# Hard-max attention: dots and picks of tiles 120 to 123 ahead of the last two maxima, four-tile dots to tile 116, fp32 dots behind the key gathers, part of the one-hots on ScalarE

## The chip, the cores and the metric

One NeuronCore of one Trainium2 chip. The metric is the device time of one execution in microseconds; lower is better. Three executions of the kernel before took 440.21, 441.21 and 441.29 us. The granted TensorE clock was 0.96 to 0.97 in every run whose time is compared here. One group of runs was granted only 0.88 to 0.92 and took over a fifth longer, the kernel before too; it is used for no comparison of times.

## The reference

```python
# q, k, v: (4, 4096, 128) fp32, standard normal
logits = np.matmul(q, k.transpose(0, 2, 1))
best = np.argmax(logits, axis=-1)
return v[b_idx, best, :]
```

No softmax: each query takes the one row of `v` whose key has the largest product. So the kernel need not compute the products exactly; it has to find the right key.

## The kernel before

The 16384 queries are 128 tiles of 128 rows. For each tile a screen in fp16 runs over all keys, with matmuls on TensorE, `Abs` and `Relu` on ScalarE, and two VectorE instructions, `fold` (W, 1.30 us) and `top` (MAX8, 1.22 us). It gives the group of four keys that holds the largest product. The rest finds the key within the group:

- `gather` computes the index (`cand`), and GpSimd fetches the three key differences of each row by an indirect DMA (`kg`), one for each tile.
- `dots` multiplies and sums them on VectorE (`prod`, `p`, `D`), for two or four tiles at once.
- `pick` takes the best (`win`), with five small VectorE instructions for a chunk of tiles.
- `put_values` puts an indirect gather of `v` rows (`vr`) in the list of late gathers, one for each tile, and a store behind every fourth.

```python
def gather(c, t0, n):
    ...
    nc.vector.tensor_scalar(out=x, in0=TOP.bitcast(U32)[:, t0:t0 + n, 0], ...)          # cand
    for j in range(n):
        near_q.append(lambda j=j: nc.gpsimd.indirect_dma_start(out=kg[:, j]..., in_=k16[t0 // NQT],
                                                               in_offset=IOA(ap=x[:, j:j + 1], axis=0)))
    ...
def dots(c, x, m):
    ...
    for i in range(0, m, h):                                                           # h = 2 tiles
        nc.vector.tensor_tensor(out=prod[:, i:i + h], in0=kg[:, i:i + h], in1=natq..., op=OP.mult)
        yield gap
    nc.vector.tensor_tensor(out=p1, in0=prod[:, :, :, 0:64], in1=prod[:, :, :, 64:128], op=OP.add)
    yield gap
    nc.vector.tensor_tensor(out=p2, in0=p1[:, :, :, 0:32], in1=p1[:, :, :, 32:64], op=OP.add)
    yield "dve",
    nc.vector.tensor_reduce(out=d[:, x - c0:x - c0 + m, 1:4], in_=p2, axis=AX_X, op=OP.add)
```

At the end rows whose answer the screen leaves in doubt are packed together: `posn` gives their places, six one-hot matrices and six matmuls move their records (`fq_e`), from which come the group indices `gb_e` and the row `row_e`. Then three gathers of whole key groups in fp32 (FK) and one of queries (FQ), twelve exact products, a last gather of values (FV) and a scatter into the output, which has to wait for the last store. The last two tiles get whole fp32 dots at once (`xk`, `dots_whole`, `win_w`).

```python
def flags_last(t0, t1, ready, fill, late):
    ...
    for z in range(SLOTS):                                     # one-hots, SLOTS = 6
        nc.vector.tensor_scalar(out=OH[:, z], in0=iota_h, scalar1=posn[:, z:z + 1], ..., op0=OP.is_equal)
    for s in range(SLOTS):
        nc.tensor.matmul(out=ps2[:, 0:6], lhsT=OH[:, s, :], rhs=rec6[:, s, :], ...)
    fill()                                                     # dots_whole(0)
    ...                                                        # gb_e, rs_e, row_e
    late(LATE)                                                 # LATE pending value gathers
    get(FK[:, 0, :], ...); get(FQ, ...)
    for r in (1, 2): get(FK[:, r, :], ...)
    yield
    ...                                                        # exact dots, the remaining late gathers
    get(FV, v_flat, win, B * Sk)
    nc.gpsimd.indirect_dma_start(out=out_flat, out_offset=IOA(ap=rowk, axis=0), in_=FV, ...)

screen(T); top(T - 2); gathers(T - 2); flush()
fold(T - 1); late_now(1); top(T - 1); gathers(T - 1); flush()
end = flags_last(T // 2, T, last_picks, lambda: dots_whole(0), late_now)
next(end)
dots_whole(1); pick_whole()
for _ in end: pass
```

GpSimd takes its gathers in the order in which the program lists them; an index that is not ready holds up all that stand behind it.

Of the kernel before, what the change touches and what calls it, by code (L numbers as in the profile page):

```python
# [8 lines left out]
FP16 = mybir.dt.float16  # L9
# [6 lines left out]
OP = mybir.AluOpType  # L16
AF = mybir.ActivationFunctionType
# [4 lines left out]
TAU = 8.0  # L22
NEAR = 0.5
SLOTS = 6
LATE = 5
NKG = 6


# [1 line left out]
def kernel(ctx, tc, q, k, v, out):  # L30
    nc = tc.nc
    B, Sq, D = q.shape
    Sk = k.shape[1]
    P = 128
    NQT = Sq // P
    T = B * NQT
# [14 lines left out]
    fp = ctx.enter_context(tc.tile_pool(name="flag", bufs=1))  # L51
# [9 lines left out]
    kd = bp.tile([P, 2, 4, 3, P], FP16, name="kd", tag="kd")  # L61
# [18 lines left out]
    def put_first(b, h):  # L80
        if b >= B:
            return
        src = natk[b % 2][:, h].rearrange("p (g f) d -> p g f d", f=4)
        nc.vector.tensor_scalar(out=kd[:, h, :, 0, :], in0=src[:, :, 0, :], scalar1=-1.0, scalar2=None, op0=OP.mult)
        kb16 = k16[b].rearrange("(r x) d -> r (x d)", x=4).rearrange("(h p g) (f d) -> p h g f d", h=2, p=P, f=3)
        for f in range(3):
            nc.sync.dma_start(out=kb16[:, h, :, f, :], in_=kd[:, h, :, 0, :])
# [57 lines left out]
    iota_h = cp.tile([P, P], FP16, tag="iota_h")  # L145
# [5 lines left out]
    for h in range(2):  # L151
# [3 lines left out]
                            op0=OP.mult, op1=OP.add)  # L155
# [72 lines left out]
    def dpart(t, x):  # L228
        if t >= T:
            return  # L230
        ps = pp.tile([P, 1024], FP32, tag="u", name=f"pd_{t}_{x}")
        mm(ps, t, 1 + 2 * x, True)
        A = ep.tile([P, 1024], FP16, tag=f"A{x}", name=f"A_{t}_{x}")
        nc.scalar.activation(out=A, in_=ps, func=AF.Abs)  # L234
        A_t[t, x] = A

    def spart(t, x):
        if t < 0:
            return
        ps = pp.tile([P, 1024], FP32, tag="u", name=f"psn_{t}_{x}")  # L240
        mm(ps, t, 2 * x, False)
        A = A_t.pop((t, x))
        for n in range(2):
            nc.tensor.matmul(out=ps[:, n * 512:(n + 1) * 512], lhsT=identh, rhs=A[:, n * 512:(n + 1) * 512], start=False, stop=True)  # L244
        if x == 0:
            E = ep.tile([P, 1024], I16, tag="E", name=f"E_{t}")
            nc.scalar.activation(out=E, in_=ps, func=AF.Relu, scale=QSCALE)  # L247
            E_t[t] = E
        else:
            E_t[t] = (E_t[t], ps)  # L250

    def screen(t):
        dpart(t, 0)
        spart(t - 1, 0)
        dpart(t, 1)
        spart(t - 1, 1)
# [6 lines left out]
    def top(t):  # L263
        nc.vector.max(out=TOP[:, t, :], in_=W_t[t % NW].bitcast(FP32))  # L264
# [88 lines left out]
    def put_rec(t0, t1):  # L353
        nc.sync.dma_start(out=rec.rearrange("(p t) w -> p t w", t=T)[:, t0:t1, :], in_=TOP.bitcast(U32)[:, t0:t1, :])
# [111 lines left out]
    def flags_last(t0, t1, ready, fill, late):  # L466
# [18 lines left out]
        for r in range(1, 4):  # L485
# [5 lines left out]
                                op0=OP.is_ge, op1=OP.mult)  # L491
        posn = fp.tile([P, SLOTS], FP32, tag="posn", name="posn_e")
# [2 lines left out]
                                       scalar=-2.0 * Sk, in1=e8[:, 1:4, 0:SLOTS].rearrange("p r s -> p s r"),  # L495
                                       op0=OP.mult, op1=OP.add)
        OH = fp.tile([P, SLOTS, P], FP16, tag="OHe", name="OH_e")
        for z in range(SLOTS):
            nc.vector.tensor_scalar(out=OH[:, z], in0=iota_h, scalar1=posn[:, z:z + 1], scalar2=None, op0=OP.is_equal)
        ps2 = pp.tile([P, 1024], FP32, tag="u", name="fq_e")  # L500
        for s in range(SLOTS):
# [9 lines left out]
        def get(dst, src, idx, hi):  # L511
            nc.gpsimd.indirect_dma_start(out=dst, out_offset=None, in_=src, in_offset=IOA(ap=idx, axis=0),
                                         bounds_check=hi - 1, oob_is_err=False)

        late(LATE)
        get(FK[:, 0, :], k_flat, gb[:, 0:1], B * Sk)
# [39 lines left out]
    def gather_whole(t):  # L556
        i = t - (T - 2)
        if i == 0:
            X_t["c"] = sp.tile([P, 2], U32, tag="xc", name="xc", bufs=1)
        c = X_t["c"][:, i:i + 1]  # L560
        nc.vector.tensor_scalar(out=c, in0=TOP.bitcast(U32)[:, t:t + 1, 0], scalar1=IDX, scalar2=IDX | (B - 1) * Sk,
                                op0=OP.bitwise_and, op1=OP.bitwise_xor)
        kk = X_t[i] = fp.tile([P, 512], FP32, tag=f"xk{i}", name=f"xk{i}")
        near_q.append(lambda: nc.gpsimd.indirect_dma_start(out=kk, out_offset=None, in_=k_flat, in_offset=IOA(ap=c, axis=0)))

    def dots_whole(i):
        for f in range(4):
            pr = fp.tile([P, P], FP32, tag="xp", name=f"xp_w_{i}_{f}", bufs=2)
            nc.vector.tensor_tensor_reduce(out=pr, in0=X_t[i][:, f * P:(f + 1) * P], in1=q32[:, i, :], scale=1.0, scalar=0.0,
                                           op0=OP.mult, op1=OP.add, accum_out=XD[:, i, f:f + 1])  # L570
# [112 lines left out]
    chunks = list(zip(cuts[:-1], cuts[1:]))  # L683
# [3 lines left out]
    def start(g, kind, c=None):  # L687
        live.append({"g": g, "kind": kind, "c": c, "wake": 0, "until": None, "n": 0})
# [40 lines left out]
    def take_late(n):  # L729
        while n > 0 and late_q:  # L730
            g = late_q.pop(0)
            n -= g not in stores
            g()
        while late_q and late_q[0] in stores:
            wait_q.append((clock[0] + 2, late_q.pop(0)))
# [3 lines left out]
    def put_out(now):  # L739
        while wait_q and wait_q[0][0] <= now:  # L740
            wait_q.pop(0)[1]()

    def issue(it):
        n = 0
        clock[0] = it
        put_out(it)
        behind = len([g for g in near_q if g not in marks]) > (2 if it >= TAIL else 4)
        while near_q and (n < 1 + behind or near_q[0] in marks or it >= T - 1):
            g = near_q.pop(0)
            n += g not in marks  # L750
            g()
        if fast and it >= rest[0]:
            fast.pop(0)()
            rest[0] = it + 2
            n += 1
        if it < 16:
            take_late(2 if n == 0 and len(late_q) > 4 else 1)
            return
        b, qt = it // NQT, it % NQT
        busy = 0.7 if qt % 2 == 0 and (10 <= qt < 18 and b + 1 < B or 18 <= qt < 26 and b + 2 < B) else 0.0  # L760
        if qt in (13, 17) and b + 1 < B:
            busy += 1.0
        rate = 2.45 if it < 72 else 2.65 if it < 80 else 2.45 if it < 96 else 2.6 if it < 104 else 2.45 if it < 112 else 2.6
        room[0] = min(room[0] + rate - busy, 3.0) - n
        for i in range(2):
            if room[0] >= 1 and late_q and it < T - 1:
                take_late(1)
                room[0] -= 1
# [3 lines left out]
    def gathers(t):  # L772
        if t >= T - 2:
            gather_whole(t)
        for c, (t0, t1) in enumerate(chunks):
            m = 4 if t1 <= 108 else 2
            if t0 <= t < t1 and t < T - 2 and (t - t0) % m == m - 1:
                gather(c, t - m + 1, m)
            if t == t0 and t < T - 2:
                start(pick(c, t0, t1), "pick", c)  # L780
        if t % 8 == 7:
            put_rec(t - 7, t + 1)
        if t == SEGS[1] - 1:
            last = [c for c, x in enumerate(chunks) if x[1] == t + 1][0]
            start(flag_segment(0, t + 1, lambda: ("cnt", last) in done, lambda: ("out", last) in done), "flags")
# [3 lines left out]
    for b in range(1, B):  # L789
        x = b * NQT  # L790
        units += [(x - 1, x - NQT + (6 + 3 * i // 2 if b == 1 else 1 + 2 * i), unit_k, b, i) for i in range(16)]
    for it in range(T):
        b, qt = it // NQT, it % NQT
# [26 lines left out]
        if it % NQT in (9, 13):  # L820
            put_first(it // NQT + 1, it % NQT // 13)
# [8 lines left out]
        if it >= 2:  # L830
            gathers(it - 2)
        issue(it)

    def flush():
# [3 lines left out]
    def late_now(n):  # L838
        take_late(n)
        put_out(1 << 20)  # L840

    def drain(group):
        for s in group:
            while True:
                try:
                    y = next(s["g"])
                except StopIteration:
                    live.remove(s)
                    break
                if y[0] == "until":  # L850
                    assert y[1]()

    def left(kind):
        return [s for s in live if s["kind"] == kind]

    screen(T)
    top(T - 2)
    gathers(T - 2)
    flush()
    fold(T - 1)  # L860
    late_now(1)
    top(T - 1)
    gathers(T - 1)
    flush()
    assert not left("flags") and not fast

    def last_picks():
        drain(left("dots"))
        drain(left("pick"))

    end = flags_last(T // 2, T, last_picks, lambda: dots_whole(0), late_now)
    next(end)
    dots_whole(1)
    pick_whole()
    for _ in end:
# [32 lines left out]
```

## Time and profile before

| | kernel before |
|---|---|
| time, three runs | 440.21, 441.21, 441.29 us |
| VectorE, ScalarE, TensorE busy | 93%, 86%, 87% of the span |
| GpSimd busy | 70%, with 0.30 us between any two gathers |
| first FK gather (called S below) | 419.12 us |
| last value gather (second `win_w`) | 428.29 us |
| last scatter | 433.66 us |

The prediction below shows the lines for these. Two more views are needed later. First the GpSimd timeline of the kernel before near tile 108; columns are start, length, engine, line, operation, and in brackets the idle time before and what ended it.

```profile
358.51 1.00 POOL L342 DMA_INDIRECT vr<-in_v_dram,win  x1 [0.30 <-issue]
359.81 0.95 POOL L282 DMA_INDIRECT kg<-k,cand  x1 [0.30 <-DVE cand L276]
...
366.59 0.96 POOL L282 DMA_INDIRECT kg<-k,cand  x1 [0.65 <-DVE cand L276]
```

A gather occupies the queue for 0.95 us (`kg`) or 1.00 us (`vr`), plus the gap of 0.30. Anything beyond 0.30 in the brackets is time that the queue lost. Second, the end of the chain of waits in the kernel before (start, length, what):

```profile
428.29 2.52 DMA vr<-in_v_dram,win_w
...
430.89 1.78 DMA out_dram<-vr
```

The last value gather lands 2.52 us after its start; its store takes 1.78 us; then comes the scatter.

### The profile page before, as it was taken

How to read it: one execution, taken by the hardware profiler on the slowest of the kernel's cores; microseconds unless marked ns; L12 is line 12 of the kernel's file. 1: busy time of each engine (PE TensorE's matmuls, PEld its weight loads, DVE VectorE, ACT ScalarE, POOL GpSimd, SP SyncE). 2: the span in 40 equal slices, each digit the busy share in tenths (PEclk: the TensorE clock that was granted, in tenths of full speed). 3: DMA queues.
4: the chain of work that ended last, by engine and by line, in shares of the span. 5: the costliest groups of instructions: out<-in, count | busy, mean ns of one | idle time of the engine just before them, and what ended most of it. 6: DMA issues, size and time to landing. Idle time of an engine off the chain costs nothing.

```text
span 437.9 us, 6167 instructions
## 1 busy us (share of the span) xinstructions
PE 378.8 (87%) x1830; PEld 168.2 (38%) x1830; DVE 407.8 (93%) x734; ACT 375.5 (86%) x437; POOL 304.9 (70%) x335
## 2 busy tenths in 40 slices
PE   8999999999999999999999889989889888896010
PEld 4444444444444444444444334434333333332010
DVE  2688999999999999999999999999999999999971
ACT  2899999999999999999999789999998988896000
POOL 8513466677757886777777776777777777777773
PEclk9999999999999999999999999999999999999555
DMA  7943999463325999763326985362322332233341
GB/s 124 198 107 67 152 151 149 97 120 86 107 66 130 167 168 188 125 123 103 89 82 150 166 154 115 91 144 81 113 81 82 89 90 84 87 101 99 106 131 55
DMA packets 52868, 50.54 MB, mean 115 GB/s; under 512 B 34136, under 2 KB 40890, under 8 KB 52832
## 3 DMA queue, kind: packets, MB, share of 16 engines
q0 software_dynamic: 19072, 33.87, 38.5%
q1 hardware_dynamic: 33760, 16.26, 14.9%
q8 instruction: 14, 0.23, 0.2%
q14 instruction: 22, 0.18, 0.1%
HBM read 40.05 MB, written 14.55 MB: 125 GB/s over the span
## 4 chain that ended last, share of the span: by engine, by line
ACT 41%; issue 19%; DVE 16%; PE 14%; DMA 6%; POOL 3%; POOLq 0%; ACTq 0%; DVEq 0%; SPq 0%
ACT A L234 34%; ACT E L247 7%; DVE TOP L264 6%; PE psn L225 5%; PE psn L244 4%; DVE W L260 4%; PE pd L225 4%; DMA natk<-in_k_dram 2%; DMA FK<-in_k_dram,gb_e 2%; DMA out_dram<-vr 1%; DVE prod L300 1%; POOL vr L342 1%; POOL kg L282 1%; DVE p L305 1%; DVE D L310 1%
## 5 line engine op out<-in xcount | busy, mean ns | idle before, releaser
L234 ACT ACTIVATE A<-pd 128x1024 f16<-128x1024 f32 x256 | 260.2, 1045 | 13.7 <-PE pd L225 13.4
L282 POOL DMA_INDIRECT kg<-k,cand x126 | 125.5, 996 | 80.1 <-DVE cand L276 49.3
L260 DVE SCALAR_TENSOR_TENSOR W<-psn,E 128x1024 int16<-128x1024 f32 x128 | 166.2, 1298 | 7.2 <-ACT E L247 5.2
L225 PE MATMUL psn<-kT,qT 128*128 128x512 f16 x512 | 151.9, 378 | 13.8 <-ACT A L234 6.0
L225 PE MATMUL pd<-kT,qT 128*128 128x512 f16 x512 | 151.9, 378 | 8.9 <-ACT A L234 8.6
L225 PEld LDWEIGHTS <-qT 128*128 128x128 f16 x1024 | 97.9, 97 | 154.0 <-issue 64.0
L264 DVE MAX8 TOP<-W 128x8 f32<-128x1024 f32 x128 | 155.9, 1218 | 0.0
L342 POOL DMA_INDIRECT vr<-in_v_dram,win x126 | 125.2, 994 | 40.4 <-issue 33.5
L244 PE MATMUL psn<-A,identh 128*128 128x512 f16 x512 | 152.0, 378 | 0.0
L247 ACT ACTIVATE E<-psn 128x1024 int16<-128x1024 f32 x128 | 132.4, 1034 | 3.3 <-PE psn L244 3.0
L244 PEld LDWEIGHTS <-identh 128*128 128x128 f16 x512 | 49.6, 97 | 60.8
L300 DVE TENSOR_TENSOR prod<-kg,natq 128x768 f16<-128x768 f16 x63 | 34.4, 546 | 0.0
L205 ACT ACTIVATE kT<-uk 128x256 f16<-128x256 f32 x48 | 20.5, 427 | 1.5 <-PE uk L202 1.5
L305 DVE TENSOR_TENSOR p<-prod 128x768 f16<-128x768 f16 (+1 forms) x36 | 17.9, 497 | 0.1
L310 DVE TENSOR_REDUCE D<-p 128x12 f32<-128x384 f16 (+1 forms) x36 | 17.5, 486 | 0.1
L201 PE MATMUL uk<-identh,natk 128*128 128x128 f16 x96 | 15.8, 218 | 0.0
L484 PE MATMUL fp_e<-n_e,tri 128*128 128x1 f32 x2 | 0.6, 348 | 13.7 <-DVE n_e L482 13.7
L202 PEld LDWEIGHTS <-natk 128*128 128x128 f16 x96 | 9.3, 97 | 7.1 <-issue 4.7
L66 POOL DMA_DIRECT2D natk<-in_k_dram x19 | 11.3, 600 | 0.8 <-POOLq L892 0.8
L308 DVE TENSOR_TENSOR p<-p 128x384 f16<-128x384 f16 (+1 forms) x36 | 11.6, 322 | 0.3
L201 PEld LDWEIGHTS <-natk 128*128 128x128 f16 x96 | 9.4, 98 | 5.6
L69 POOL DMA_DIRECT2D natq<-in_q_dram x15 | 9.1, 612 | 0.0
(152 smaller groups left out, 140.2 us busy)
## 6 DMA issues: line engine op xcount, KB each, us to landing
out_dram<-vr SPq DMA_DIRECT2D x31, 256.0 KB, 2.2
natq<-in_q_dram POOLq DMA_DIRECT2D x12, 256.0 KB, 6.8
natk<-in_k_dram POOLq DMA_DIRECT2D x10, 256.0 KB, 4.6
k<-kd SPq DMA_DIRECT2D x18, 128.0 KB, 3.4
k<-natk POOLq DMA_DIRECT2D x6, 384.0 KB, 6.6
kg<-k,cand POOLq DMA_INDIRECT x126, 2.7
vr<-in_v_dram,win POOLq DMA_INDIRECT x126, 2.6
natk<-in_k_dram POOLq DMA_DIRECT2D x8, 128.0 KB, 5.2
```

Source lines behind the costliest of these rows:

```text
L201: nc.tensor.matmul(out=o, lhsT=natk[b % 2][:, h, 4 * m + x, :], rhs=identh, start=True, stop=False)
L225: nc.tensor.matmul(out=ps[:, n * 512:(n + 1) * 512], lhsT=qT[b % 2][:, qt * P:(qt + 1) * P], rhs=kT[b % 2][:, u * 1024 + n * 512:u * 1024 ...
L234: nc.scalar.activation(out=A, in_=ps, func=AF.Abs)
L244: nc.tensor.matmul(out=ps[:, n * 512:(n + 1) * 512], lhsT=identh, rhs=A[:, n * 512:(n + 1) * 512], start=False, stop=True)
L247: nc.scalar.activation(out=E, in_=ps, func=AF.Relu, scale=QSCALE)
L260: nc.vector.scalar_tensor_tensor(out=W_t[t % NW].bitcast(I16)[:, 1::2], in0=ps, scalar=QSCALE, in1=E, op0=OP.mult, op1=OP.max)
L264: nc.vector.max(out=TOP[:, t, :], in_=W_t[t % NW].bitcast(FP32))
L282: near_q.append(lambda j=j: nc.gpsimd.indirect_dma_start(out=kg[:, j].rearrange("p f d -> p (f d)"), out_offset=None, in_=k16[t0 // NQT], ...
L300: nc.vector.tensor_tensor(out=prod[:, i:i + h], in0=kg[:, i:i + h], in1=natq[b % 2][:, x + i - b * NQT:x + i + h - b * NQT, :].unsqueeze(2 ...
L305: nc.vector.tensor_tensor(out=p1, in0=prod[:, :, :, 0:64], in1=prod[:, :, :, 64:128], op=OP.add)
L310: nc.vector.tensor_reduce(out=d[:, x - c0:x - c0 + m, 1:4], in_=p2, axis=AX_X, op=OP.add)
L342: late_q.append(lambda j=j: nc.gpsimd.indirect_dma_start(out=vr[:, j, :], out_offset=None, in_=v_flat, in_offset=IOA(ap=win[:, i + j:i + j ...
```

## The change

Its intent: VectorE is full until 405 us, and behind 419 us a chain of gathers decides. So take some work off VectorE, get the winners of tiles 120 to 123 early so that the GpSimd queue doesn't wait for them, let one value gather fewer stand between FK and FV, and shorten the way from `posn` to `row_e`.

```diff
-LATE = 5
+LATE = 4
@@ put_first (kd)
+        if b == B - 1:
+            nc.scalar.activation(out=kd[:, h, :, 0, :], in_=src[:, :, 0, :], func=AF.Copy, scale=-1.0)
+        else:
             nc.vector.tensor_scalar(out=kd[:, h, :, 0, :], in0=src[:, :, 0, :], scalar1=-1.0, ...)
@@ flags_last
-        for z in range(SLOTS):
+        far = fp.tile([P, 2, P], FP16, tag="far", name="far_e")
+        for z in (SLOTS - 2, SLOTS - 1):
+            w = far[:, z - SLOTS + 2]
+            nc.scalar.activation(out=w, in_=iota_h, func=AF.Abs, scale=-1.0, bias=posn[:, z:z + 1])
+            nc.scalar.activation(out=OH[:, z], in_=w, func=AF.Relu, scale=-1.0, bias=1.0)
+        for z in range(SLOTS - 2):
             nc.vector.tensor_scalar(out=OH[:, z], ...)
@@ issue
+        if it == T - 1:
+            take_late(1)
@@ gathers
-            m = 4 if t1 <= 108 else 2
+            m = 4 if t1 <= 116 else 2
@@ end of the program
     screen(T)
+    drain([x for x in left("dots") if x["c"] == len(chunks) - 3])
+    drain(left("pick")[:1])
+    late_now(1)
     top(T - 2)
@@
-    end = flags_last(T // 2, T, last_picks, lambda: dots_whole(0), late_now)
+    end = flags_last(T // 2, T, last_picks, lambda: None, late_now)
     next(end)
+    dots_whole(0)
     dots_whole(1)
```

More of the change, by code (lines that the diff above doesn't have):

```diff
@@ L83, in put_first @@
         src = natk[b % 2][:, h].rearrange("p (g f) d -> p g f d", f=4)
-        nc.vector.tensor_scalar(out=kd[:, h, :, 0, :], in0=src[:, :, 0, :], scalar1=-1.0, scalar2=None, op0=OP.mult)
+        if b == B - 1:
+            nc.scalar.activation(out=kd[:, h, :, 0, :], in_=src[:, :, 0, :], func=AF.Copy, scale=-1.0)
+        else:
+            nc.vector.tensor_scalar(out=kd[:, h, :, 0, :], in0=src[:, :, 0, :], scalar1=-1.0, scalar2=None, op0=OP.mult)
         kb16 = k16[b].rearrange("(r x) d -> r (x d)", x=4).rearrange("(h p g) (f d) -> p h g f d", h=2, p=P, f=3)
```

## The prediction

> **What bounds the kernel now.** I read the engine totals first, then the busy time of single stretches, then the GpSimd queue's timeline of the last quarter, then the end instruction by instruction.
>
> ```profile
> PE 378.8 (87%) x1830; PEld 168.2 (38%) x1830; DVE 407.8 (93%) x734; ACT 375.5 (86%) x437; POOL 304.9 (70%) x335
> ```
>
> VectorE is busiest. The stretches say where (columns: stretch, sum, then busy time of PE, weight loads, DVE, ACT, POOL, clock, DMA share, GB/s):
>
> ```profile
> 100.00:200.00 100.00, 97.89 (x480) 43.73 (x479) 100.00 (x144) 99.54 (x121) 74.26 (x77) 1.00 0.64 127
> 360.00:405.00 45.00, 36.68 (x155) 14.72 (x152) 44.38 (x86) 36.44 (x39) 33.51 (x34) 1.00 0.31 91
> 419.10:437.90 18.80, 0.59 (x2) 0.50 (x2) 6.77 (x52) 0.00 (x0) 10.05 (x10) 0.50 0.34 98
> ```
>
> Until 405 us VectorE is full (from 20 to 410 us its waits sum to 4.5 us). TensorE and ScalarE end near 402 us. After 419 us no engine is full: a chain of gathers decides.
>
> POOL's 33.51 of 45 us looks like slack and is not. The timeline (start, length, [idle before <- releaser]):
>
> ```profile
> 391.44 1.00 POOL L342 DMA_INDIRECT vr<-in_v_dram,win  x1 [0.31 <-issue]
> 392.74 0.96 POOL L282 DMA_INDIRECT kg<-k,cand  x1 [0.30 <-issue]
> 394.00 1.00 POOL L342 DMA_INDIRECT vr<-in_v_dram,win  x1 [0.30 <-issue]
> ...
> 405.23 0.96 POOL L282 DMA_INDIRECT kg<-k,cand  x1 [1.15 <-DVE cand L276]
> ...
> 413.80 1.01 POOL L342 DMA_INDIRECT vr<-in_v_dram,win  x1 [1.23 <-DVE near L323]
> ...
> 419.12 1.05 POOL L512 DMA_INDIRECT FK<-in_k_dram,gb_e  x1 [0.41 <-DVE row_e L509]
> ...
> 423.08 0.99 POOL L512 DMA_INDIRECT FK<-in_k_dram,gb_e  x1 [0.31 <-issue]
> 424.38 1.00 POOL L342 DMA_INDIRECT vr<-in_v_dram,win  x1 [0.30 <-DMA FQ<-in_q_dram,row_e]
> 425.68 1.00 POOL L342 DMA_INDIRECT vr<-in_v_dram,win  x1 [0.30 <-issue]
> ...
> 428.29 1.00 POOL L342 DMA_INDIRECT vr<-in_v_dram,win_w  x1 [0.30 <-issue]
> 429.59 1.00 POOL L512 DMA_INDIRECT FV<-in_v_dram,xw_fe  x1 [0.30 <-issue]
> 433.66 1.02 POOL L541 DMA_INDIRECT out_dram<-FV,rowk_e  x1 [3.08 <-DMA out_dram<-vr]
> ```
>
> An idle of 0.30 (or 0.31) is the queue's own gap: a gather costs 1.26 us (kg) or 1.30 us (vr). Counting from the kg at 353.44 us to FK at 419.12 us, 49 gathers take 65.68 us, and only five waits exceed 0.30: by 0.35 (366.59), 0.17 (373.29), 0.85 (405.23), 0.93 (413.80) and 0.11 (419.12), together 2.4 us. So the queue is a second bound almost level with VectorE: if VectorE gets faster, at most 2.4 us can be won before FK.
>
> The end, with S = 419.12 us the start of the first FK gather:
>
> ```profile
> 418.95 0.15 DVE L509 TENSOR_SCALAR row_e<-rs_e 128x1 uint32<-128x1 f32 x1
> 427.23 0.29 DVE L594 CUSTOM_DVE_ANT_0 xp_fe<-FK,FQ 128x128 f32<-128x128 f32 x1 [1.01 <-DMA FK<-in_k_dram,gb_e]
> 428.88 0.17 DVE L607 TENSOR_REDUCE xw_fe<-xl_fe 128x1 uint32<-128x12 f32 x1
> ```
>
> FV needs xw_fe, which ends at 429.05 = S+9.93; but FV starts at S+10.47, because eight gathers stand ahead of it (8 x 1.309). So behind S the queue decides, not the dots. The last scatter starts at S+14.54: it waits for the store of the last two tiles, whose second gather starts at S+9.17, lands 2.52 later and whose store ends near S+13.7.
>
> **What the Trainium skill says.** "DMA: Bandwidth & Descriptors", section "Latency and other measured facts", gives about 1 us to first byte on the GpSimd path, from the emission of descriptors; the trace agrees (0.95 to 1.05 us on POOL), and shows that this time holds the queue. The same page, "Anatomy of one DMA — SWDGE (gpsimd) path", fits 2.0 us plus bytes/436e3: 2.15 us for a vr (64 KB), 2.6 us for an FK (256 KB). The trace shows 2.6 and 4.0 from issue to landing; I use these. "ScalarE: Activation LUTs", section "What ACT_TABLE_LOAD costs", gives 186 ns + 0.833 ns per element, some 93 ns more for a per-partition pointer operand, and 2.66 us for a change of table set. The trace agrees with the first (1034 ns for 1024 elements). Abs, Relu and Copy all run there already, so I expect no table load.
>
> **The change, part by part.**
>
> *Negation of kd on ScalarE, last batch.* Two VectorE instructions go, at 228.86 and 242.14 us. Each lasts 0.27 us, but the next starts 0.20 us later, so 0.4 us is saved. ScalarE gets two of about 186 + 512 x 0.833 = 612 ns (estimate from the page). It is full at 229 us but waits 0.46 us near 236, and 1.07 us near 243, and the following stretches have 8 of 10 us busy. I count 0.3 us.
>
> *Four-tile dots for tiles 108 to 115.* By start-to-start spacing, a two-tile tail costs add 0.37, second add 0.18, reduction 0.25 = 0.80, four times 3.2. A four-tile tail costs 0.48 + 0.27 + 0.45 = 1.2, twice 2.4. Two index instructions fewer save 0.14; four products that no longer run just ahead of a maximum cost two more gaps of 0.12, so 0.24. Net 0.7 us. Placing every VectorE instruction of the new order by those spacings instead, I find the index of tiles 124/125 at 403.7, 1.1 us earlier than 404.79; the two workings bracket the saving, and I keep 1.1 as the most that VectorE can give.
>
> *Tiles 120 to 123 earlier.* Nothing is removed; dots and pick (2.35 us of VectorE) move from behind the last maxima to ahead of them. What it gives is to the queue: the win of these tiles is there by 406 instead of 413.5 us, so the 0.93 us wait at 413.80 goes; three gathers instead of two precede the kg of 124, so the 0.85 at 405.23 goes too. And one of the two value gathers of 124/125 now stands ahead of FK: behind the last xk come three of group 120 to 123 and one of 124/125, where before came one of 116 to 119 and four of 120 to 123.
>
> *Dots of tile 126 behind FK's start.* L569's first four cost 4 x 0.21 = 0.84 us of VectorE between the one-hots (end 417.92) and gb_e (418.69). The six matmuls end near 418.2, so 0.3 us at most is freed.
>
> *One-hots 4 and 5 on ScalarE.* VectorE saves 2 x 0.17 = 0.34 us. ScalarE needs Abs, Relu, Abs, Relu: 280 + 107 = 387 ns with a pointer bias and about 300 ns without (estimates from the page), some 1.3 us plus the hand-over, against 1.08 us for all six on VectorE. So this eats the 0.3 us: net zero at row_e.
>
> **The sum.** VectorE alone would have row_e 1.1 + 0.3 = 1.4 us earlier, near 417.7. The queue: 50 gathers instead of 49 ahead of FK at (65.68 - 2.4)/49 = 1.291 us = 64.55, plus a new wait. Three vr now precede the kg of tile 108, which comes free at 358.6 us, but its index is ready, as now, only at 359.07 + 0.44 = 359.5: 0.85 us lost. Another 0.1 at tile 122. So FK at 353.44 + 65.5 = 418.9, less the 0.3 of kd (the queue waited 1.32 us for VectorE at 322.06, so it follows): 418.6. By adding the ideal 1.26 and 1.30 I get 418.2. I take 418.5, a gain of 0.6 us, and the queue, not VectorE, sets it.
>
> Behind FK: seven gathers ahead of FV instead of eight, 7 x 1.309 = S+9.16. Now xw_fe at S+9.93 decides (its FK2 is issued and lands as before; VectorE has 1.08 us idle at 424.42 for the 0.84 us of moved dots). FV starts near S+10.0, lands 2.45 later, S+12.45. The last pair's second gather starts at S+7.85, its store ends at S+12.4. The scatter, 0.83 us after the later one, starts at S+13.3 instead of S+14.54: gain 1.25 us. In total 0.6 + 1.25 = 1.85 us: 441.2 becomes 439.4 us.
>
> **Rivals.** (1) *VectorE sets FK*: the gain ahead is 1.4 us, total 2.65, 438.6 us. For it: its 44.38 of 45 us. Against: the queue's five waits of only 2.4 us, and one gather more. (2) *The queue gains nothing ahead*, as four-tile groups deliver indices in bursts and it starves more than once: 0.3 us lost, total 1.0, 440.2 us. For it: the waits at 283.63 and 322.06 us, where four-tile groups run. (3) *ScalarE's one-hots come late*, by a table load or slow dependent steps: 2.7 us on the path, less the queue's slack of 0.8, so 441.3 us. Against: the same functions run all along. (4) *Slower because ScalarE is late at 229 us*: up to 0.6 us, 440 us.
>
> **Range and chances.** The runs before spread over 440.21 to 441.29 us, and the rivals over 438.6 to 441.3. The mean lies near 439.4; 80% in 437.9 to 440.8. Two per cent is 8.8 us, several times the whole sum: within 2% is nearly certain.
>
> **What would show it.** In the changed profile: FK starts between 418 and 419 us, its idle before is 0.30 (queue) rather than a longer wait for row_e (then rival 1); the wait ahead of the kg of tile 108 near 359 us is over 1 us; no wait over 0.4 us for win behind 405 us; FV starts about 10.0 us behind FK with about 1.1 us idle ahead of it; the scatter 13.3 us behind FK; four ACT instructions of 0.3 to 0.4 us and no table load. A scatter that still starts 14.5 us behind FK, or FK at 419 or later, would make it wrong.

## The result, and the profile after

| | before | after |
|---|---|---|
| time, four runs each (of before the three above and one more) | median 440.71 us (440.14 to 441.29) | median 439.65 us (439.26 to 439.82) |
| ratio of after to before | | 0.9975, 95% interval 0.9956 to 0.9993 |
| S, the first FK gather | 419.12 | 419.62 |
| `row_e` done | 419.10 | 418.44 |
| last value gather | 428.29 = S+9.17 | 427.54 = S+7.92 |
| FV | 429.59 = S+10.47 | 429.62 = S+10.00 |
| last scatter | 433.66 = S+14.54 | 433.66 = S+14.04 |

A ratio is here the mean time of one kernel's fast runs over that of the other's in the same rounds, so not quite the ratio of the medians that are quoted. The result is about 1.1 us faster, a quarter of a per cent, with an interval that excludes zero. But the four times of the kernel before lie at two levels (440.14 and 440.21, 441.21 and 441.29): the changed kernel's median is 0.5 us under the lower and 1.6 us under the upper, so that the size of the gain depends on the draw. The predicted 439.4 us lies close to it, and the range held. But the way there is not the predicted one: FK starts 0.5 us *later* than before, not 0.6 earlier.

The engine totals of the changed kernel:

```profile
PE 377.8 (86%) x1830; PEld 168.0 (38%) x1830; DVE 406.6 (93%) x722; ACT 377.3 (86%) x443; POOL 304.9 (70%) x335
```

VectorE has 12 instructions and 1.2 us less. ScalarE has six instructions and 1.8 us more. The number of gathers is unchanged. The same stretches as in the prediction (stretch, sum, then busy time of PE, weight loads, DVE, ACT, POOL, clock, DMA share, GB/s):

```profile
360.00:405.00 45.00, 35.80 (x153) 14.52 (x150) 44.14 (x80) 36.04 (x38) 34.33 (x36) 1.00 0.32 91
419.60:437.90 18.30, 0.59 (x2) 0.50 (x2) 6.58 (x50) 0.00 (x0) 9.15 (x9) 0.50 0.34 97
```

GpSimd has 36 instead of 34 gathers between 360 and 405 us: it is ahead. The GpSimd timeline of the changed kernel:

```profile
359.10 0.96 POOL L285 DMA_INDIRECT kg<-k,cand  x1 [1.20 <-DVE cand L279]
...
370.68 1.30 POOL L345 DMA_INDIRECT vr<-in_v_dram,win  x1 [0.31 <-DVE prod L303]
...
381.20 1.22 POOL L345 DMA_INDIRECT vr<-in_v_dram,win  x1 [0.30 <-issue]
382.72 1.23 POOL L285 DMA_INDIRECT kg<-k,cand  x1 [0.30 <-issue]
...
406.29 0.96 POOL L285 DMA_INDIRECT kg<-k,cand  x1 [0.31 <-DVE near L326]
...
411.37 1.38 POOL L345 DMA_INDIRECT vr<-in_v_dram,win  x1 [0.30 <-issue]
413.06 0.95 POOL L572 DMA_INDIRECT xk<-in_k_dram,xc  x1 [0.30 <-DVE D L313]
414.31 1.09 POOL L345 DMA_INDIRECT vr<-in_v_dram,win  x1 [0.30 <-issue]
...
419.62 1.01 POOL L520 DMA_INDIRECT FK<-in_k_dram,gb_e  x1 [0.30 <-DVE XD L577]
...
427.54 1.03 POOL L345 DMA_INDIRECT vr<-in_v_dram,win_w  x1 [0.30 <-issue]
429.62 1.00 POOL L520 DMA_INDIRECT FV<-in_v_dram,xw_fe  x1 [1.05 <-DVE xw_fe L615]
433.66 1.02 POOL L549 DMA_INDIRECT out_dram<-FV,rowk_e  x1 [3.04 <-DMA out_dram<-vr]
```

Three things are to be seen. The waits at 405 and 413 us are gone (every gather there starts 0.30 or 0.31 us behind the one before), and a wait of 0.90 us beyond the gap stands at 359.10, at tile 108. The idle before FK is exactly the gap of 0.30, so FK comes when the queue reaches it and not when `row_e` is ready. And some gathers last 1.22 to 1.38 us instead of 0.95 to 1.01: nothing in the brackets shows this loss, because it is in the length.

Below, two of the VectorE instructions that run when the first of these long gathers starts, and, much later, `gb_e` and `row_e`; both from the VectorE timeline of the changed kernel.

```profile
369.97 0.54 DVE L303 TENSOR_TENSOR prod<-kg,natq 128x768 f16<-128x768 f16 x1
370.55 0.56 DVE L308 TENSOR_TENSOR p<-prod 128x768 f16<-128x768 f16 x1
...
418.03 0.16 DVE L513 TENSOR_SCALAR gb_e<-fq_e 128x3 uint32<-128x3 f32 x1 [0.91 <-PE fq_e L510]
418.29 0.15 DVE L517 TENSOR_SCALAR row_e<-rs_e 128x1 uint32<-128x1 f32 x1
```

The gather of 370.68 starts 0.13 us into the add of 370.55. And VectorE idles 0.91 us before `gb_e`. The end of the chain of waits after:

```profile
427.54 2.86 DMA vr<-in_v_dram,win_w
...
430.49 2.19 DMA out_dram<-vr
```

The last value gather starts 0.75 us earlier than before, but landing and store took 5.05 us instead of 4.30, and in this pair of profiles the whole 0.75 is lost again. Both profiled executions have a span of 437.9 us. One execution is one draw: the profiled one of the kernel before took 439.86 us, less than any of its executions in the runs that follow (20 of them, the fastest 439.94), while that of the changed kernel took its median. So this pair of profiles can't be used for the difference in time; it can be used for the order of events.

### The profile page after: what moved, and what is told of

It reads as the page before. It is cut to its first block, busy times and chain, and to the rows that moved or that the text cites. A ratio compares the mean times of both kernels' runs of the same rounds, so it can differ in the third digit from the quotient of the medians.

```text
span 437.9 us, 6162 instructions
## 1 busy us (share of the span) xinstructions
PE 377.8 (86%) x1830; PEld 168.0 (38%) x1830; DVE 406.6 (93%) x722; ACT 377.3 (86%) x443; POOL 304.9 (70%) x335
## 4 chain that ended last, share of the span: by engine, by line
ACT 44%; PE 21%; issue 17%; DVE 11%; DMA 5%; POOL 2%; POOLq 0%; ACTq 0%; DVEq 0%; SPq 0%
ACT A L237 35%; ACT E L250 9%; PE psn L228 8%; PE psn L247 6%; PE pd L228 6%; DVE TOP L267 4%; DVE W L263 3%; DMA vr<-in_v_dram,win 2%; DMA natk<-in_k_dram 2%; POOL vr L345 1%; DVE prod L303 1%; DMA vr<-in_v_dram,win_w 1%; DVE p L308 1%; DMA out_dram<-vr 0%; DVE p L311 0%
```

## The experiments

The theory after the result had three parts. (A) What counts is the time that the GpSimd queue loses between two gathers, by waits and by longer gathers; moving a gather from behind FK to ahead of it shifts FK but not the last value gather. (B) The longer gathers are those that start while VectorE multiplies or adds fp16 pairs; four-tile dots bring such pairs to where the gathers start. (C) The short landing of the last value gather in the profile of before was chance. Rivals: that the change itself slows the landings (against C), that ScalarE's one-hots or the moved fp32 dots put FK later (against A), and that a gather's length has nothing to do with VectorE (against B).

### First group, five rounds: the change again, its halves, one value gather more

`again` is the changed kernel, unchanged. `early_only` is the kernel before with only the early part:

```diff
-LATE = 5
+LATE = 4
+        if it == T - 1:
+            take_late(1)
     screen(T)
+    drain([x for x in left("dots") if x["c"] == len(chunks) - 3])
+    drain(left("pick")[:1])
+    late_now(1)
```

`no_early` is the changed kernel without these lines; `kd`, four-tile dots, ScalarE's one-hots and the place of the dots of tile 126 stay as changed. `rate1` is the changed kernel with one value gather more ahead of the keys of tile 108, to cover the new wait:

```diff
-        rate = ... 2.6 if it < 104 else 2.45 if it < 112 else 2.6
+        rate = ... 2.6 if it < 104 else 2.65 if it < 112 else 2.6
```

> The changed kernel once more, for the spread of its trace. Queue theory (the GpSimd gather queue sets the start of the first FK gather): FK starts at 419.3 to 419.9 us with only the usual 0.30 us ahead of it, row_e done about 1 us before; FV 10.0 us and the last scatter about 14.0 us behind FK; 1.0 us faster than the kernel before. VectorE theory (row_e sets FK): FK follows row_e within 0.2 us.

> The kernel before with only the early dots and picks of tiles 120 to 123 and the gather that moves ahead of FK. No VectorE work is saved. Queue theory: the two waits of 0.85 and 0.93 us go, FK at 418.9 to 419.4, the scatter 14.0 instead of 14.5 us behind it, so 0.6 to 1.0 us faster than before: most of what the whole change gave. VectorE theory: row_e is not earlier, FK at 419.1, 0.3 us at most is won.

> The changed kernel without that part, with all its VectorE savings. Queue theory: the parts do not add up; FK at 417.9 to 418.6, scatter 14.5 us behind it, 0.5 to 1.1 us faster than before, so that the two halves together are worth more (1.5 to 2) than the whole (1.06). VectorE theory: the savings of 1.0 to 1.4 us are passed on in full and the halves add up to the whole: then this one is 0.8 to 1.0 us faster and the early part alone 0.0 to 0.3.

> The changed kernel with one value gather more put in the queue before the index of tile 108 is ready, so that the wait of 0.89 us near 359 us (and some of the 0.65 near 347) is filled. Nothing changes on VectorE. Queue theory: FK 0.7 to 1.1 us earlier than in the repeat, until row_e at 418.4 becomes the bound, and the time 0.6 to 1.0 us shorter than the repeat's. VectorE theory: row_e is where it was, no change (0.2 us).

Measured, with the kernel before at a median of 440.16 us (nine runs):

| | median us | ratio to before | 95% interval | S | last value gather | FV |
|---|---|---|---|---|---|---|
| again | 440.02 | 0.9985 | 0.9972 to 0.9999 | 419.73 | 427.64 | S+10.15 |
| early_only | 439.88 | 0.9991 | 0.9977 to 1.0004 | 419.76 | 427.62 | S+10.12 |
| no_early | 439.39 | 0.9983 | 0.9968 to 0.9997 | 418.40 | 427.63 | S+10.53 |
| rate1 | 439.55 | 0.9985 | 0.9971 to 0.9999 | 419.25 | 427.06 | S+9.74 |

All four were correct. By time alone the four can't be told apart: the intervals overlap, and the whole change gained 0.7 us here instead of 1.1. The traces tell more. The GpSimd timeline of `early_only`, then of `no_early`:

```profile
419.76 1.05 POOL L512 DMA_INDIRECT FK<-in_k_dram,gb_e  x1 [0.64 <-DVE row_e L509]
...
427.62 1.00 POOL L342 DMA_INDIRECT vr<-in_v_dram,win_w  x1 [0.30 <-issue]
```

```profile
413.19 1.01 POOL L345 DMA_INDIRECT vr<-in_v_dram,win  x1 [0.83 <-DVE near L326]
...
418.40 1.02 POOL L520 DMA_INDIRECT FK<-in_k_dram,gb_e  x1 [0.31 <-DVE row_e L517]
...
427.63 1.00 POOL L345 DMA_INDIRECT vr<-in_v_dram,win_w  x1 [0.31 <-issue]
```

FK differs by 1.36 us between the two, which is one gather more ahead of it, and still the last value gather starts at the same time to 0.01 us, in the whole change too. Each half brings 0.66 to 0.67 us at this place, and both together bring no more (0.65 in this repeat). In `early_only` FK waits for `row_e`: without the saved VectorE work the queue arrives first. In `no_early` the wait for `near` is back at 413 us (0.53 us beyond the gap), as the theory wants it.

`rate1` did remove the wait at 359 us, but it came back later, 0.89 us at 391.55 and 0.17 at 398.24: the list of winners is empty there, and a gather taken earlier is missing later. The last value gather still starts 0.58 us earlier than in `again`; the time shows nothing of it that the interval could separate.

The expectations missed in several places: `early_only` has FK at 419.76 us (418.9 to 419.4 expected) and gains 0.4 us instead of 0.6 to 1.0; in `no_early` the scatter starts 15.77 us behind FK, not 14.5; in `rate1` FK is 0.48 us earlier than in `again`, not 0.7 to 1.1.

On (C): in these four profiles landing and store of the last value gather sum to 5.13 to 5.51 us. The chain of `again`:

```profile
427.64 3.18 DMA vr<-in_v_dram,win_w
430.90 2.29 DMA out_dram<-vr
```

That is 5.47 us for the same kernel that showed 5.05 in its first profile. `early_only` has the last pair's gathers and store as in the kernel before and shows 5.51, not 4.30. So the 4.30 us from the kernel before was at the short end of a spread of over 1 us. The spread also shows in the times: of the nine profiled executions of the two kernels and the variants of this group and the next, the three that took over 440 us (`again`, `early_only`, `no_early`) are the three with 5.46 to 5.51 us here, and the six below 440 us have 4.30 to 5.13. That it makes the two levels of the times is likely from this, and not tested.

### Second group: one part undone at a time, and the disputed cost by itself

`no_quads` sets the limit for four-tile dots back, `onehot_dve` puts all six one-hots on VectorE again, `fill_back` puts the dots of tile 126 back ahead of `gb_e`; all else stays as changed. The edits, in this order:

```diff
-            m = 4 if t1 <= 116 else 2
+            m = 4 if t1 <= 108 else 2
```
```diff
-        for z in (SLOTS - 2, SLOTS - 1):        # Abs and Relu on ScalarE
-            ...
-        for z in range(SLOTS - 2):
+        for z in range(SLOTS):
```
```diff
-    end = flags_last(T // 2, T, last_picks, lambda: None, late_now)
+    end = flags_last(T // 2, T, last_picks, lambda: dots_whole(0), late_now)
     next(end)
-    dots_whole(0)
```

`phases` adds to the kernel before, behind its end, six phases of eight gathers each. VectorE meanwhile does nothing, 20 products of the size of `prod` into one buffer, nine maxima, 40 scalings of 384 elements, the products again, and nothing.

```diff
+    PH = (("none", 0), ("mult", 20), ("max", 9), ("scale", 40), ("mult", 20), ("none", 0))
+    for p, (kind, n) in enumerate(PH):
+        ...                                    # waits for the phase before
+        for j in range(8):
+            nc.gpsimd.indirect_dma_start(out=GD[:, j, :], ..., in_=v_flat, in_offset=IOA(ap=cx, axis=0))
+        for j in range(n):
+            if kind == "mult":
+                nc.vector.tensor_tensor(out=SO, in0=SA, in1=natq..., op=OP.mult)      # 128 x 768 fp16
+            elif kind == "max":
+                nc.vector.max(out=S8, in_=W_t[0].bitcast(FP32))
+            else:
+                nc.vector.tensor_scalar(out=SO[:, 0]..., in0=SA[:, 0]..., scalar1=-1.0, ..., op0=OP.mult)
```

> The changed kernel with two-tile dots again for tiles 108 to 115. Queue theory: the 0.90 us wait near 359 us goes and the small ones of the kernel before (0.3 and 0.2) are back; row_e is 0.7 to 1.1 us later (419.2 to 419.6) and now level with the queue, FK at 419.2 to 419.8, the time within 0.4 us of the repeat of the changed kernel. VectorE theory: 0.7 to 1.1 us slower than the repeat.

> The changed kernel with all six one-hots on VectorE. From the changed kernel's trace, VectorE stands idle 0.91 us for ScalarE's two; six on VectorE would end at 417.46, 0.3 us ahead of ScalarE's 417.75. So row_e is 0.2 to 0.3 us EARLIER than with the move, and, as the queue is 1.2 us behind row_e, FK does not move: same time as the repeat within 0.3 us. Rival (the move to ScalarE helps): row_e 0.3 us later.

> The changed kernel with the fp32 dots of tile 126 back ahead of the key gathers. They fall into the 0.91 us in which VectorE waits for ScalarE, so row_e is at most 0.1 us later, FK does not move, and the time is the repeat's within 0.3 us. VectorE theory: 0.84 us later row_e and time.

> The kernel before with six phases added behind its end, eight value gathers each, while VectorE does nothing, 20 fp16 products of the dots' shape, maxima of 1024, 40 fp16 scalings of 384, products again, nothing. Theory of the stretched gathers (a gather that meets a VectorE instruction with two SBUF inputs is held up): about 0.95 to 1.0 us each in the idle phases and under the maxima, 1.10 to 1.40 under the products. Rival (the long gathers come from other DMA traffic): the same 0.95 to 1.0 in all six. The time is some 60 us longer; the output is the same.

Measured, with the kernel before at a median of 441.09 us (eleven runs; they fall into two levels near 440.2 and 441.2, as above):

| | median us | ratio to before | 95% interval | S | last value gather | landing + store |
|---|---|---|---|---|---|---|
| no_quads | 439.07 | 0.9958 | 0.9946 to 0.9971 | 419.00 | 426.92 | 4.84 us |
| onehot_dve | 439.42 | 0.9967 | 0.9954 to 0.9980 | 419.54 | 427.35 | 4.92 us |
| fill_back | 439.43 | 0.9966 | 0.9953 to 0.9980 | 419.72 | 427.59 | 4.77 us |

**Four-tile dots cost time.** `no_quads` is the fastest kernel, 0.35 us under its two companions of the same rounds (their intervals overlap; the changed kernel itself did not run in these rounds). Its GpSimd timeline:

```profile
419.00 1.11 POOL L520 DMA_INDIRECT FK<-in_k_dram,gb_e  x1 [0.46 <-DVE row_e L517]
...
426.92 1.03 POOL L345 DMA_INDIRECT vr<-in_v_dram,win_w  x1 [0.30 <-issue]
```

VectorE has more to do now, and FK waits 0.16 us for `row_e`; even so FK and the last value gather start 0.62 us earlier than in the changed kernel's profile. (`row_e` is done at 418.99 us, ahead of the expected 419.2 to 419.6, and so is FK.)

**The one-hots on ScalarE don't count.** In `onehot_dve` VectorE idles less before `gb_e`, as its timeline shows:

```profile
417.65 0.16 DVE L508 TENSOR_SCALAR gb_e<-fq_e 128x3 uint32<-128x3 f32 x1 [0.28 <-PE fq_e L505]
```

The way from `posn` to `row_e` takes 1.80 us with all six on VectorE and 2.10 with two on ScalarE, so the hand-over costs 0.30 us. In both kernels FK starts more than 1 us after `row_e`, so nothing of this reaches FK. `fill_back` shows the other side: the four fp32 dots fit into the gap that the wait for ScalarE leaves (`posn` to `row_e` 2.11 us with them, 2.10 without).

**The gathers by themselves: the first try failed.** In `phases` every gather lasted 0.94 to 1.02 us, under the products too. As it was put, the expectation is refuted. The timeline of one of its product phases:

```profile
454.94 5.55 DVE L893 TENSOR_TENSOR SO<-SA,natq 128x768 f16<-128x768 f16 x9
...
456.81 0.94 POOL L890 DMA_INDIRECT GD<-in_v_dram,cx  x1 [0.30 <-issue]
458.06 0.94 POOL L890 DMA_INDIRECT GD<-in_v_dram,cx  x1 [0.30 <-issue]
```

Nine products take 5.55 us, 0.62 each. They all write one buffer, so each waits for the one before it, and every second one starts 0.03 to 0.04 us before a gather. In the kernel the next instruction starts 0.47 us after a product. So the test was not like the kernel. It was not without contact, though, which the trace shows one instruction at a time: the products that a gather met in this way lasted 0.62 us and the others 0.56, and in the phase of the scalings one in four, the one that runs while a gather ends, lasted 0.32 to 0.33 us against 0.26. Here the gathers passed, and VectorE lost 0.06 to 0.07 us each time.

### What 1448 gathers show

The nine profiles of the kernels before, after and the seven variants of these two groups hold 1448 gathers between 200 and 420 us. Sorted by where they start relative to an fp16 product or add of 768 elements on VectorE:

| a gather starts | number | length |
|---|---|---|
| up to 0.10 us before it | 37 | 17 of 0.94 to 1.01, 20 of 1.37 to 1.63 us |
| 0.02 to 0.10 us into it | 8 | 1.31 to 1.41, mean 1.36 us |
| 0.10 to 0.20 us | 64 | 1.16 to 1.31, mean 1.24 us |
| 0.20 to 0.35 us | 46 | 1.01 to 1.24, mean 1.12 us |
| later in it | 103 | mean 0.98 us |
| none of these | 1190 | mean 0.97 us, 9 of them over 1.1 |

The length falls by as much as the start comes later: about 1.4 us minus the offset. So a gather of 0.95 or 1.00 us is held until some 0.4 us after the product began, shortly before the next VectorE instruction starts (0.47 us after it). Products and adds of this size are not the only ones: of the nine in the last row two start just over 0.10 us ahead of one (1.47 and 1.48 us), two beside the negation of `kd` on VectorE (1.23 and 1.24), and five beside smaller two-input instructions in fp32 (1.10 to 1.19).

### Third group: slow, and one look at the better test

`again2`, `before_again` and `two_back_rate` (four-tile dots back to 108, all one-hots on VectorE, and the value gather of `rate1`) were to settle whether the changed kernel lands its last values more slowly, and whether a version beats `no_quads`. `phases2` repeats `phases` with a mix like that of the kernel: a maximum, then two products into different buffers.

```diff
-    PH = (("none", 0), ("mult", 20), ("max", 9), ("scale", 40), ("mult", 20), ("none", 0))
+    PH = (("none", 0), ("mix", 5), ("max", 10), ("mix", 6), ("mult", 22))
...
+            if kind in ("max", "mix"):
+                nc.vector.max(out=S8_t[j % 2], in_=W_t[0].bitcast(FP32))
+            for i in range({"max": 0, "mix": 2, "mult": 1}[kind]):
+                nc.vector.tensor_tensor(out=SO_t[(i + j) % 2], in0=SA, in1=natq..., op=OP.mult)
```

> The changed kernel, as the yardstick of this chip and of the runs below: FK 419.5 to 419.8 us, queue idle 0.30 ahead of it, the long gathers near 370.7, 381, 382.6 and 411.4 us again; 0.7 to 1.6 us faster than the kernel before.

> The changed kernel with two parts taken back (two-tile dots for tiles 108 to 115, all one-hots on VectorE) and one value gather more put in the queue near tile 105. Theory: row_e 418.5 to 418.8, the queue no later, FK 418.5 to 418.9 with no long wait in the queue behind 340 us; 0.3 to 0.9 us faster than the repeat of the changed kernel. Rival (the four-tile dots and the move to ScalarE help): 0.5 to 1.0 us slower.

> The kernel before once more, for the landing times behind FK. Theory (the profile of before was a lucky one: the last value gather took 2.52 us to land and its store 1.78, together 4.30, where seven other kernels' profiles have 4.8 to 5.5): FK at 418.9 to 419.6, the last value gather issued 9.2 us behind it, landing and store together 4.7 to 5.6, so the scatter 14.9 to 15.8 us behind FK. Rival (the change itself slows these transfers): 4.2 to 4.5 again.

> Gathers under VectorE work once more, now in the loop's own order: a maximum, then two products into different buffers, so that products start without waiting for one another. If a gather is held when it starts inside a product (about 1.42 us less the time since the product's start, in the traces of nine kernels), gathers that start 0.02 to 0.35 us into a product last 1.07 to 1.40 us here too, and those under maxima 0.94. If it is something else of the main loop (TensorE, ScalarE, other transfers), all stay at 0.94 to 1.02.

The chip was slow for this whole group: the kernel before took 527.96 to 548.02 us (median 542.76), `again2` 545.91, `two_back_rate` 541.37, `before_again` 539.47. Nothing is concluded from these times, and neither question is settled by them. `phases2` (612.05 us) is still of use, since in its phases TensorE is not in use and a gather without VectorE work lasts 0.95 us, as on the other chip. Its timeline, both engines, in the first mixed phase and in the maxima behind it:

```profile
558.11 0.95 POOL L890 DMA_INDIRECT GD<-in_v_dram,cx  x1 [0.31 <-issue]
...
560.57 1.00 DVE L895 TENSOR_TENSOR SO<-SA,natq 128x768 f16<-128x768 f16 x2
560.64 1.29 POOL L890 DMA_INDIRECT GD<-in_v_dram,cx  x1 [0.30 <-issue]
...
564.70 1.00 DVE L895 TENSOR_TENSOR SO<-SA,natq 128x768 f16<-128x768 f16 x2
564.76 1.76 POOL L890 DMA_INDIRECT GD<-in_v_dram,cx  x1 [0.31 <-issue]
...
573.59 0.94 POOL L890 DMA_INDIRECT GD<-in_v_dram,cx  x1 [0.30 <-issue]
```

A gather that starts beside a maximum lasts 0.94 to 0.96 us. One that starts 0.07 us into a pair of products lasts 1.29, one held over both 1.76. The second mixed phase repeats this with 1.28 and 1.76. With products back to back and alternating buffers all gathers but the first last 1.10 to 1.11. So the products do lengthen the gathers, in a test that holds nothing else; that `phases` failed because its products left a gap is argued from the spacing (0.62 us against 0.47 in the kernel) and not shown.

### The account of the queue

From the 56th gather before the last value gather to that one, the nine kernels have the same gathers, 19 of them `kg`. Their time can be split: what goes beyond the gap of 0.30 is waiting, what goes beyond 0.95 (`kg`, `xk`) or 1.00 us (all others) is lengthening (both counted from the traces).

| | from | last value gather | waiting | lengthening | rest |
|---|---|---|---|---|---|
| before | 353.44 | 428.29 | 2.41 | 0.44 | 72.00 |
| after | 353.02 | 427.54 | 0.90 | 1.47 | 72.15 |
| again | 353.12 | 427.64 | 0.90 | 1.38 | 72.24 |
| early_only | 353.85 | 427.62 | 0.82 | 0.82 | 72.13 |
| no_early | 353.11 | 427.63 | 1.43 | 0.89 | 72.20 |
| rate1 | 352.43 | 427.06 | 1.06 | 1.46 | 72.11 |
| no_quads | 353.03 | 426.92 | 0.75 | 1.04 | 72.10 |
| onehot_dve | 352.89 | 427.35 | 0.81 | 1.58 | 72.07 |
| fill_back | 353.07 | 427.59 | 0.75 | 1.69 | 72.08 |

The rest is the same to 0.24 us in all nine. The change removed 1.51 us of waits and put 1.03 us of longer gathers in their place. Without the four-tile dots the waits stay as low, and 0.43 us of the lengthening go. That is part (A), and in part (B): the early part lengthens gathers too (0.82 in `early_only`, which has none at tiles 108 to 115, against 0.44 before; 1.47 after against 0.89 in `no_early`), since it also moves where gathers and products meet.

The table also gives the time that the 56 gathers take, from the first column to the second: 74.85 us before, 73.77 in `early_only`, 74.52 in `no_early`, 74.52 after, 73.89 in `no_quads`. This is the cleaner measure of the parts, as the first column moves by itself: `early_only` and the kernel before are the same program up to there, and are 0.41 us apart.

## Why the prediction was right or wrong

**Right.** The queue sets FK, and not VectorE: the idle before FK is 0.30 us, and `row_e` was done 1.18 us before. Rival 1 is out. The new wait at tile 108 was put at 0.85 us and is 0.90. The waits at 405 and 413 us are gone. FV was put at S+10.0 with about 1.1 us idle ahead of it; it is S+10.00 with 1.05. The `kd` move was counted as 0.3 us at 322 us; the queue is 0.27 us earlier there in this pair, and the seven kernels with it have this gather at 321.65 to 321.90 us against 322.06, 322.43 and 322.24 in `before`, `early_only` and `phases`, so rival 4 is out. The ScalarE instructions have the estimated lengths (637 ns for `kd` against 612; 394 ns for the Abs of a one-hot against 387), and there is no table load but one at the very start, so rival 3 is out. The dots of tile 126 and the one-hots were together counted as a net zero; from `posn` to `row_e` it takes 2.10 us after and 2.29 before, so 0.19 less. The one-hots alone cost 0.30 us; the dots' move gives 0.49 with all one-hots on VectorE (2.29 against 1.80 in `onehot_dve`) and nothing with two on ScalarE. The queue hides all of it.

**Wrong, the first term: "So FK at 353.44 + 65.5 = 418.9, less the 0.3 of kd ...: 418.6", taken as 418.5.** FK came at 419.62, by the prediction's own test ("FK at 419 or later would make it wrong") a failure. The term that was mis-sized is the cost of one gather: 1.291 us were taken from the kernel before, and the changed kernel, its wait taken off, shows (66.60 - 0.90)/50 = 1.314 us. Times 50 this is 1.15 us. Gathers longer than 1.01 us between 360 and 421 us exceed it by 1.24 us together, against 0.25 in the kernel before. The prediction treated the length of a gather as a constant that VectorE cannot touch; it counted what the four-tile dots save on VectorE (0.7 to 1.1 us) and nothing of what they cost GpSimd, nor that the early part brings new meetings of gathers and products.

A page that the prediction did not look up has a cause that fits. The Trainium skill, "SBUF — State Buffer", section "Who interferes with whom", says that a VectorE instruction with two SBUF inputs contends with a GpSimd instruction that reads SBUF, and that the pair of ports is an exclusive lock which the first to issue keeps for the whole instruction. `prod` and `p` have two SBUF inputs; MAX8 has one, and W takes one of its two from PSUM. An indirect gather takes its row numbers (`cand`, `win`) from SBUF. The table of 1448 gathers agrees: held until some 0.4 us after the product began (the profile gives a product 0.54 us), and not held by MAX8 (0.94 to 0.96 us in `phases2`). `phases` agrees with the lock from the other side: there the gather passed and the product lasted 0.06 us longer. That the row numbers are what the held gather reads is argued, not shown.

VectorE missed its mark too: `row_e` was expected "near 417.7" and was done at 418.44. The index of tiles 124/125 is ready 0.71 us earlier than before, and this holds `kd`. So the lower of the two workings of the four-tile dots was the right one, and the prediction kept the higher, 1.1. It made no difference, as the queue decided.

**Wrong, the second term: "The scatter, 0.83 us after the later one, starts at S+13.3 instead of S+14.54: gain 1.25 us".** It started at S+14.04; in the repeat of the same kernel at S+14.45. The last value gather did start at S+7.92 (predicted S+7.85). What failed is the landing and the store behind it, some 4.5 us in the prediction, of which 2.52 is a single profile's landing. Measured were 5.05 and 5.47. In all nine profiles these two steps sum to 4.30 to 5.51 us, and the kernel before itself has more than 4.30 in another trace (see "Open"). A step with such a spread can't be taken from one execution, and the 1.25 us of gain had it as a constant.

**Why the time fits all the same.** The predicted last value gather is 418.5 + 7.85 = 426.35 us; it came at 427.54, 1.2 us late. The measured gain is 1.1 us in the first comparison and 0.7 in the second, instead of 1.85, and the base was an uncertain draw: 441.2 us is the median of three runs; one more run (440.14) made it 440.71, and the later groups have 440.16 and 441.09. A base that was 0.5 us above that of the comparison and a gain that was 0.8 us too large met at 439.4 against 439.65. That the number was right is in part luck.

**Why the parts don't add up.** Rival 2 said that the queue would gain nothing ahead of FK and give 1.0 us in total. Its time was nearest to the gain that was measured, and its mechanism was half right: the queue starves once more, at 359 us, but mainly it lengthens. Each half of the change starts the last value gather 0.66 to 0.67 us earlier; the whole (0.65 and 0.75) does hardly better. Counted over the 56 gathers alone, the early part by itself gains 1.08 us and the other half 0.33, but the whole only 0.33 too, and 0.96 without the four-tile dots. So the other half, of which the four-tile dots are the part that acts here, gains 0.33 us on its own, by fewer waits; beside the early winners, which save most of these waits already, the four-tile dots cost 0.63, of which 0.43 is longer gathers and 0.15 waiting. The rest of the 0.75 (0.42 us) comes from ahead of 353 us. All this rests on one profile of each kernel.

**Open.** Whether the changed kernel lands its last values more slowly than the one before, beyond chance, was to be settled in the group that ran slow. A trace of the group before it bears on this: up to its end `phases` is the kernel before, unchanged, and ran there at the usual pace (S at 419.31 us). Its tail:

```profile
428.59 1.00 POOL L342 DMA_INDIRECT vr<-in_v_dram,win_w  x1 [0.30 <-issue]
429.89 1.00 POOL L512 DMA_INDIRECT FV<-in_v_dram,xw_fe  x1 [0.30 <-DVEq L625]
435.09 1.03 POOL L541 DMA_INDIRECT out_dram<-FV,rowk_e  x1 [4.20 <-DMA out_dram<-vr]
```

From the start of the last value gather to the scatter it takes 6.50 us, against 5.37 in the profile of `before` and 6.12 and 6.54 in the two of the changed kernel. So the kernel before lands as slowly as the changed one in some executions; 4.30 us was a short draw, and nothing asks for a slower landing by the change. How often each kernel draws which is open. Whether `two_back_rate` beats `no_quads` is open too, as both ran slow. `no_quads` beats the kernel before (0.9958); against the changed kernel there is only the comparison with its two companions, which differ from the change in one part each (0.9967 and 0.9966).

## What to carry to other kernels

When an engine's queue works through a fixed list, count what it loses between two marks, as waits *and* as longer instructions; moving an item from one side of a mark to the other shifts the mark and wins nothing. The length of an indirect gather is not a constant: look at what VectorE does when it starts, and be careful with long two-input VectorE instructions in a stretch where GpSimd has no slack. And a step of the last chain that rests on one DMA's landing should be read from several executions before a gain of its size is promised.

## What the Trainium skill lacked or had wrong

- "SBUF — State Buffer", section "Who interferes with whom", has the rule that fits the longer gathers, but infers in the same section that `tensor_tensor` does not stall GpSimd DMAs, since making descriptors needs the write side. For indirect gathers the runs show the opposite: 1.31 to 1.41 us instead of 0.95 when the gather starts right behind a 128x768 fp16 product, up to 1.76 when it is held over two.
- The same section says that the first to issue keeps the pair; it does not say how soon a gather asks for it. In `phases`, gathers that started 0.03 to 0.04 us into a product lasted 0.94 us (and the product 0.06 longer), while in the kernels gathers that started up to 0.10 us *ahead* of a product lasted up to 1.63 us.
- "DMA: Bandwidth & Descriptors", section "Anatomy of one DMA — SWDGE (gpsimd) path", calls the making of descriptors small and variable; the 1 us to first byte that the prediction quotes from the same page is the better guide. A gather of 128 rows holds the GpSimd queue for 0.95 to 1.05 us, plus 0.30 us to the next if VectorE does not lengthen it, whether a row has 512 bytes (`vr`), 768 (`kg`) or 2 KB (FK); this rate bounds the last quarter of the kernel. Its fit (an estimate from it: 2.15 us for 64 KB) was too short for the last value gather, which landed after 2.5 to 3.7 us in nine profiles.
